# A tuned two-network transformer kernel whose instruction order is set with the timeline simulator's timing model

## The chip, the cores and the metric

The kernel runs on one core of one Trainium2 chip. The time is that of one execution on the device, in microseconds (us). A core has five engines that run side by side, each its own list of instructions in a fixed order: TensorE for matrix products (PE; its weight loads are PEld), VectorE (DVE), ScalarE (ACT), GpSimd (POOL) and SyncE (SP), which here issues nearly all transfers from the chip's memory (DMA). An engine that reaches an instruction whose input is not there yet stands still; it never takes a later one first. So the order in each list is a part of the program.

## The reference, cut to what matters

A sequence of 256 rows of 1024 numbers goes through two networks, one after the other, in fp32.

```python
def first_block(x, positions, ...):            # two layers
    for i in range(DEPTH):
        x = x + 0.5 * swiglu_ffn(x, ffn1_norm[i], ffn1_w_gate[i], ffn1_w_up[i], ffn1_w_down[i])
        h = rmsnorm(x, mix_norm[i])
        if i % 2 == 0:
            x = x + even_mixer(h, ...)         # chunked gMLP; attention over compressed,
        else:                                  # selected and windowed keys
            x = x + odd_mixer(h, ...)          # attention over indexed keys; attention over blocks
        x = x + 0.5 * swiglu_ffn(x, ffn2_norm[i], ...)
    return rmsnorm(x, final_norm)

def second_block(x, c, ...):
    mod = silu(c) @ w_ada + b_ada
    h = modulate(rmsnorm_2(x, g_mix), sh1, sc1)
    proj = h @ w_in
    y_a = rwkv7_time_mix(h, proj[..., :o1], ...)
    y_b = rglru_branch(proj[..., o1:o2], proj[..., o2:o3], ...)
    merged = sigmoid(proj[..., o3:o4]) * (y_a @ p_a) + sigmoid(proj[..., o4:]) * (y_b @ p_b)
    x = x + gt1 * (merged @ w_out)
    h2 = modulate(rmsnorm_2(x, g_ffn), sh2, sc2)
    x = x + gt2 * hier_moe(h2, ...)            # 32 experts, two for each row
    return modulate(rmsnorm_2(x, g_final), shf, scf)
```

In the RG-LRU branch the gates are `gate_r = sigmoid(...)` and `gate_i = sigmoid(...)`, and the input of the recurrence carries `sqrt(-expm1(2.0 * log_a))`: tanh, exp and sqrt alternate there.

## The kernel before, in words

Activations lie transposed in SBUF, 128 features by 256 tokens in a tile. A weight matrix comes in pieces of 128x1024 or 128x2048 fp32 numbers into a stage tile `s` by a DMA on SP (line 353); ACT rounds it to a high part `h` (helper `act`, line 258), DVE forms the low part `l = s - h` (helper `tt`, line 239), and a product is three matmuls, `xh*h`, `xl*h` and `xh*l`, where `xh` and `xl` are the two parts of the activations (`mm`, line 233; `tr`, line 236, is a transpose on PE). All helpers have one line each, so a row of the profile is told apart by its tiles: `ps` is a PSUM bank, `we` an expert's weights, `con` constants.

The stages, by the times of the trace: FFN 1 of layer 0 to about 207 us; the even mixer to 345; FFN 2 and FFN 1 of layer 1 to 757; the odd mixer to 881; FFN 2 to 1076; then the second network: the input projection with the RWKV part's preparation (`rwkv_in`, lines 1337 and on) to 1197, among it the RG-LRU gates (`rglru`, lines 1307 to 1335) at 1197 to 1218; the RWKV recurrence in blocks (`rwkv_out`) to 1317; merge and output projection to 1345; router and experts (`moe_round`, line 1898) to about 1585; the last norm to 1600. Weights of the modulation (`ada`, on DVE) are folded in beside the FFNs.

In the mixers and in the second network, code of two kinds is written as generators and interleaved: latency chains (attention units, RWKV units, where each step on PE waits for ACT, DVE or POOL) and plain products of weights ("fillers"), which give PE work meanwhile. In the even mixer the fillers are `blocks` B(0) and B(1) (`ps<-s,ev_blkk` and `ps<-s,ev_blkv`), features F(4) to F(6), and gMLP (line 851).

In `rwkv_in` each of the four units starts with a product of `tw` and `w2a` and, after a chain through ACT, POOL and DVE (a norm by `pow` on POOL, then `ex4` on DVE, line 455), has `ex4` broadcast by PE, `ps<-con,ex`.

In `rglru` every channel group c has two products into banks of one tag (p1), two Tanh that read them (`gr`, `gi`), an Exp and a Tanh, and then a Sqrt of `gr` (line 1328). Sqrt stands in another table of ACT than Tanh and Exp, and a switch is an instruction of ACT, ACT_TABLE_LOAD.

The experts: their 1 MB pieces `we` are loaded by SP in the order of use, into a ring of buffers; a load whose buffer is still read by PE waits on SP. For the experts that are ordered by their number of rows, the address comes from a table `moe_idx` in SBUF, read into registers of SP ahead of the load (line 1863, in `expert_load`):

```python
            if (p, kind) not in self.where:
                self.where[p, kind] = self.nc.sync.value_load(self.idx[0:1, p:p + 1], min_val=0, max_val=NEXP - 1)
            e = bass.ds(self.where[p, kind], 1)
            src = self.A["w2e"][e].squeeze(0) if kind else self.A["w13"][e, h].squeeze(0)
```

Each such read is a TENSOR_LOAD and two register instructions behind it. 48 of them are executed.

Nothing in the kernel writes the order of a list out by hand, but for a few `issue_after` hints (as that at the end of `rglru`, which keeps the Gelu behind the last Sqrt). The program is written down as one sequence of operations with their tiles, and the framework's scheduler (`tile.TileContext`) makes the list of every engine from it: it walks through the operations with a model of how long each takes, and puts next on an engine what is ready first by that model. By default it uses its own table of costs.

## Time and profile before

| | us |
|---|---|
| median of 2 runs | 1599.16 (1596.77 and 1601.55) |
| profiled execution | 1602.33 |
| its span from first to last instruction | 1600.6 |
| PE busy | 1533.1 |
| DVE / ACT / POOL busy | 1049.0 / 696.7 / 320.6 |

The prediction rests on views of the one profiled execution. The page gives the busy time of each engine, the span in 40 slices, and the chain of work that ended last, followed back from the end. A view by windows gives, for each stretch, the time each engine was busy, with the number of its instructions, the clock that TensorE was granted (1.00 is 2.4 GHz, 0.50 is 1.2 GHz), the mean busy share of the 16 DMA engines, and the bytes per second. The waits view sums what an engine stood waiting for. A timeline lists instructions one after another (neighbours of one kind in one row, with their count), and in brackets the idle time ahead of one and what ended it. The length shown for a matmul runs to its modelled end; matmuls overlap, so that the distance from start to start is what one costs.

### The profile page before, as it was taken

What the parts mean: (1) busy time and instruction counts of PE and PEld (TensorE: products, weight loads), DVE (VectorE), ACT (ScalarE), POOL (GpSimd) and SP (SyncE); (2) the same over time, 40 slices, a digit from 0 to 9 for tenths busy, and PEclk for the clock granted to TensorE, in tenths of its full rate; (3) what the DMA queues carried; (4) which work ended last, traced back from release to release, by engine and by line L of the source; (5) the groups of instructions that cost most, each with busy time, mean ns of one, the idle gap of its engine ahead of it and who ended that gap; (6) DMA issues with size and microseconds to landing.
All of it is one profiled execution on the core that took longest, in us unless ns stands there. A gap on an engine that the chain in (4) does not pass through costs nothing.

```text
span 1600.6 us, 29956 instructions
## 1 busy us (share of the span) xinstructions
PE 1533.1 (96%) x11925; PEld 1361.7 (85%) x11925; DVE 1049.0 (66%) x1938; ACT 696.7 (44%) x1241; POOL 320.6 (20%) x338
## 2 busy tenths in 40 slices
PE   8999998999999999999999999999899999999976
PEld 8999996789999999999878999998898889644433
DVE  6777876776875667766897678757786556532212
ACT  5544444554454444444545445534456433211102
POOL 4222222132220112201221222224313013000000
PEclk9999999999999999999999999999999999999997
DMA  8675555035774657745433576536440139899995
GB/s 305 241 281 199 197 196 193 27 120 204 270 253 162 211 184 263 262 166 185 145 110 132 205 269 243 189 119 227 133 148 27 54 141 378 323 388 420 420 421 193
DMA packets 62484, 344.35 MB, mean 215 GB/s; under 512 B 11137, under 2 KB 15361, under 8 KB 28545
## 3 DMA queue, kind: packets, MB, share of 16 engines
q1 hardware_dynamic: 59520, 340.65, 57.9%
q8 instruction: 96, 1.57, 0.4%
q0 software_dynamic: 640, 1.57, 0.4%
q10 hardware_dynamic: 2176, 0.13, 0.1%
q14 instruction: 52, 0.42, 0.1%
HBM read 339.05 MB, written 2.36 MB: 213 GB/s over the span
## 4 chain that ended last, share of the span: by engine, by line
PE 71%; issue 15%; DVE 8%; POOL 2%; ACT 2%; DMA 1%; ACTq 0%; SPq 0%; DVEq 0%; POOLq 0%
PE ps L233 70%; DVE l L239 2%; PE ps L236 1%; ACT h L258 1%; DVE xl L248 1%; POOL rte L239 1%; DVE t L239 1%; POOL t L239 0%; DVE xh L243 0%; DMA s<-in_ffn_gu 0%; DMA s<-in_ev_win 0%; DVE t L248 0%; POOL sq L239 0%; POOL kne L239 0%; DVE x L239 0%
## 5 line engine op out<-in xcount | busy, mean ns | idle before, releaser
L233 PE MATMUL ps<-xh,h 128*128 128x256 f32 x1992 | 570.1, 286 | 12.3 <-ACT h L258 7.6
L233 PE MATMUL ps<-xh,l 128*128 128x256 f32 x1992 | 570.4, 286 | 0.0
L233 PE MATMUL ps<-xl,h 128*128 128x256 f32 x1992 | 568.9, 286 | 0.3
L258 ACT ACTIVATE h<-s 128x1024 fp32r<-128x1024 f32 (+4 forms) x419 | 401.5, 960 | 366.9 <-PE ps L233 289.1
L239 DVE TENSOR_TENSOR l<-s,h 128x1024 fp32r<-128x1024 f32 (+4 forms) x416 | 464.9, 1125 | 139.5 <-ACT h L258 138.3
L233 PEld LDWEIGHTS ps<-xh,h 128*128 128x128 f32 x1992 | 380.8, 191 | 17.2 <-ACT h L258 7.0
L233 PEld LDWEIGHTS ps<-xh,l 128*128 128x128 f32 x1992 | 380.8, 191 | 6.1 <-DVE l L239 2.7
L233 PEld LDWEIGHTS ps<-xl,h 128*128 128x128 f32 x1992 | 381.1, 191 | 1.4 <-DVE xl L248 0.9
L233 PE MATMUL ps<-ah,h 128*128 128x256 f32 x704 | 201.4, 286 | 0.0
L239 POOL TENSOR_TENSOR t<-t,t 128x256 f32<-128x256 f32 x93 | 121.1, 1303 | 399.6 <-DVE t L239 338.8
L233 PE MATMUL ps<-ah,l 128*128 128x256 f32 x704 | 199.3, 283 | 0.1
L233 PE MATMUL ps<-al,h 128*128 128x256 f32 x704 | 199.1, 283 | 0.0
L233 PEld LDWEIGHTS ps<-ah,l 128*128 128x128 f32 x704 | 134.9, 192 | 0.4 <-DVE l L239 0.3
L233 PEld LDWEIGHTS ps<-al,h 128*128 128x128 f32 x704 | 135.0, 192 | 0.0
L233 PEld LDWEIGHTS ps<-ah,h 128*128 128x128 f32 x704 | 134.9, 192 | 0.0
L233 PE MATMUL ps<-we,gT 128*32 128x512 f32 (+1 forms) x512 | 100.1, 610 | 7.7 <-DMA we<-in_w 7.7
L239 DVE TENSOR_TENSOR t<-ps,rb 128x256 f32<-128x256 f32 x196 | 81.9, 421 | 33.1 <-PE ps L233 25.0
L258 ACT ACTIVATE ah<-t 128x256 fp32r<-128x256 f32 x88 | 36.7, 417 | 117.6 <-POOL t L239 117.6
L239 DVE TENSOR_TENSOR al<-t,ah 128x256 fp32r<-128x256 f32 x88 | 38.0, 432 | 63.9 <-ACT ah L258 63.9
L233 PEld LDWEIGHTS ps<-we,gT 128*32 128x32 f32 (+1 forms) x512 | 26.0, 121 | 59.9 <-issue 44.7
L239 POOL TENSOR_TENSOR sa<-sa,sq 128x256 f32<-128x256 f32 x34 | 41.9, 1232 | 149.7 <-ACT sq L258 149.4
L248 DVE SCALAR_TENSOR_TENSOR ada<-s,ca,ada 128x1024 f32<-128x1024 f32 x56 | 71.5, 1278 | 0.0
(487 smaller groups left out, 2091.1 us busy)
## 6 DMA issues: line engine op xcount, KB each, us to landing
s<-in_ffn_gu SPq DMA_DIRECT2D x87, 1024.0 KB
we<-in_w SPq DMA_DIRECT2D x64, 1024.0 KB
s<-in_ffn_dn SPq DMA_DIRECT2D x64, 704.0 KB
we<-in_w2e SPq DMA_DIRECT2D x28, 1024.0 KB
s<-in_w_ada SPq DMA_DIRECT2D x24, 1024.0 KB
s<-in_w_in SPq DMA_DIRECT2D x18, 1024.0 KB
s<-in_w_ada_f SPq DMA_DIRECT2D x8, 1024.0 KB
s<-in_ev_win SPq DMA_DIRECT2D x7, 1024.0 KB
```

The costliest lines, as they stand in the source:

```text
L233: return self.nc.tensor.matmul(out, lhsT, rhs, start=start, stop=stop, skip_group_check=True)
L236: self.nc.tensor.transpose(out, in_, ident)
L239: return (eng or self.nc.vector).tensor_tensor(out, a, b, op=op)
L248: self.nc.vector.scalar_tensor_tensor(out, a, s, b, op0=op0, op1=op1)
L258: self.nc.scalar.activation(out, a, f, **kw)
```

## The change

One argument is added: the scheduler takes the time of each operation from the framework's other timing model, that of the timeline simulator, instead of its own table. The operations stay the same; their order in the lists of all five engines is made anew.

```diff
-    with tile.TileContext(nc) as tc:
+    with tile.TileContext(nc, schedule_with_timeline_sim=True) as tc:
```

PE, DVE, POOL and SP execute the same instructions as before in another order; ACT has four more, all ACT_TABLE_LOAD. Three places show how.

On PE at the start of the second network's RWKV units (`rwkv_in`): `m_tw,m_w2a` are the first products of unit 0, `xh,h`, `xl,h` and `xh,l` are products of input features that need none of it. Rows with + are the order now, with - the order before.

```order
 L233 MATMUL ps_13606<-xl_13358,h_13598 128x256
 L233 MATMUL ps_13606<-xh_13394,l_13599 128x256
+L233 MATMUL ps_13744<-m_tw,m_w2a 128x256
+L233 MATMUL ps_13750<-m_tw,m_w2a 128x256
 L233 MATMUL ps_13638<-xh_13359,h_13602 128x256
 L233 MATMUL ps_13638<-xl_13358,h_13602 128x256
@@ -8122,6 +8123,4 @@
 L233 MATMUL ps_13712<-xl_13358,h_13676 128x256
 L233 MATMUL ps_13712<-xh_13394,l_13677 128x256
-L233 MATMUL ps_13744<-m_tw,m_w2a 128x256
-L233 MATMUL ps_13750<-m_tw,m_w2a 128x256
 L233 MATMUL ps_13833<-xh_13359,h_13825 128x256
```

The two products stand 72 feature matmuls earlier. The broadcast that ends this unit's chain, `ps_13765`, stood inside the feature `ps_13833`, 25 instructions behind the products; now it stands here, behind the next feature:

```order
 L233 MATMUL ps_13859<-xl_13358,h_13829 128x256
 L233 MATMUL ps_13859<-xh_13394,l_13830 128x256
+L233 MATMUL ps_13765<-con,ex_2534_13766 128x128 x2
+L233 MATMUL ps_13819<-t_2550_13817,con 128x256
 L233 MATMUL ps_13895<-xh_13359,h_13887 128x256
 L233 MATMUL ps_13895<-xl_13358,h_13887 128x256
```

Between the second product and the broadcast lie 122 instructions of PE instead of 24. In the other three units the distance grows from 35 to 68, from 81 to 116, and from 24 to 50.

On ACT in `rglru`: `gi` and `gr` are the gates, L1328 is the Sqrt.

```order
 L258 ACTIVATE xb_13582<-gr_13574,nsp_12282 128x256
-L258 ACTIVATE gi_13578<-ps_14932,hb_igate 128x256
 L258 ACTIVATE t_2767_14937<-gr_13574,sp_12281 128x256
 L1328 ACT_TABLE_LOAD
 L1328 ACTIVATE gr_13573<-gr_13573 128x256
+L258 ACT_TABLE_LOAD
+L258 ACTIVATE gi_13578<-ps_14932,hb_igate 128x256
+L1328 ACT_TABLE_LOAD
 L1328 ACTIVATE gr_13574<-gr_13574 128x256
 L258 ACT_TABLE_LOAD
 L258 ACTIVATE gr_13575<-ps_14947,hb_rgate 128x256
```

The second gate's Tanh has moved between the Sqrt of group 0 and that of group 1, so that the table is switched four times for the two Sqrt instead of twice; the same happens a little later between groups 2 and 3.

On SP in the queue of the experts' loads, before the change:

```order
L1873 DMA we_17410<-in_w 128x2048
L1873 ISA
L1873 DMA we_17412<-in_w 128x2048
L1873 ISA
L1873 DMA we_17414<-in_w 128x2048
L1873 DMA we_17467<-in_w2e 128x2048
L1873 DMA we_17469<-in_w2e 128x2048
L1863 TENSOR_LOAD moe_idx
L1863 ISA x2
L1873 ISA
L1873 DMA we_17486<-in_w 128x2048
```

and with it, from the end of the reads between `we_17412` and `we_17469`:

```order
L1863 TENSOR_LOAD moe_idx
L1863 ISA x2
L1873 DMA we_17469<-in_w2e 128x2048
L1863 TENSOR_LOAD moe_idx
L1863 ISA x2
```

The reads, which were spread over the whole queue, come in blocks: 15 between `we_17408` and `we_17410`, 11 between `we_17412` and `we_17469`, 5 between this and `we_17414` (then `we_17467` and `we_17486`), 12 between `we_17486` and `we_17497`, one more ahead of `we_17552`; the remaining four are the first of all, and stand as before.

## Rows read from the trace of the kernel before

**Rows 1.** The page: busy time of each engine, and the chain by engine.

```profile
PE 1533.1 (96%) x11925; PEld 1361.7 (85%) x11925; DVE 1049.0 (66%) x1938; ACT 696.7 (44%) x1241; POOL 320.6 (20%) x338
PE 71%; issue 15%; DVE 8%; POOL 2%; ACT 2%; DMA 1%; ACTq 0%; SPq 0%; DVEq 0%; POOLq 0%
```

**Rows 2.** Windows: start:end, length, each engine's busy time, clock, DMA share, GB/s.

```profile
100.00:200.00 100.00, 100.00 (x836) 99.73 (x834) 76.86 (x133) 45.28 (x69) 22.57 (x14) 1.00 0.62 216
245.00:337.00 92.00, 85.23 (x607) 64.64 (x606) 67.36 (x186) 46.85 (x147) 15.75 (x17) 0.98 0.27 97
778.00:890.00 112.00, 105.61 (x797) 91.10 (x798) 93.48 (x228) 60.01 (x139) 24.68 (x26) 0.98 0.35 123
1090.00:1197.00 107.00, 99.25 (x777) 93.99 (x777) 81.10 (x171) 47.40 (x83) 32.04 (x48) 0.97 0.49 165
1197.00:1218.00 21.00, 18.75 (x101) 14.43 (x99) 16.20 (x37) 18.70 (x37) 6.55 (x15) 0.84 0.09 15
1287.00:1317.00 30.00, 29.90 (x261) 26.16 (x261) 15.12 (x48) 11.26 (x26) 4.11 (x4) 1.00 0.39 139
1317.00:1345.00 28.00, 23.82 (x181) 23.19 (x181) 20.89 (x33) 11.52 (x18) 9.46 (x8) 0.94 0.93 360
1404.00:1527.00 123.00, 121.07 (x766) 58.06 (x762) 31.68 (x80) 18.75 (x35) 0.00 (x0) 1.00 1.01 420
1527.00:1575.00 48.00, 38.61 (x213) 14.80 (x217) 8.24 (x21) 4.25 (x8) 0.00 (x0) 0.96 1.02 414
```

**Rows 3.** Timelines of ACT, DVE and PE: one weight piece in an FFN.

```profile
28.96 1.06 ACT L258 ACTIVATE h<-s 128x1024 fp32r<-128x1024 f32 x1 [0.40 <-PE ps L233]
34.57 0.28 PE L233 MATMUL ps<-xh,h 128*128 128x256 f32 x1
34.69 0.28 PE L233 MATMUL ps<-xl,h 128*128 128x256 f32 x1
```

**Rows 4.** Timeline of PE, even mixer: two neighbours of a block B.

```profile
263.62 0.38 PE L233 MATMUL ps<-s,ev_blkk 128*64 128x256 f32 x1
263.84 0.38 PE L233 MATMUL ps<-s,ev_blkk 128*64 128x256 f32 x1
```

**Rows 5.** Waits of PE at 1090 to 1197: total, times, longest.

```profile
PE ps L233 <- DVE ex L455: 6.2, 4, 1.8
```

**Rows 6.** Timeline of PE there, unit 0, and a window behind such a wait.

```profile
1103.69 0.70 PE L233 MATMUL ps<-m_tw,m_w2a 64*128 64x256 f32 x4
1109.72 0.68 PE L233 MATMUL ps<-con,ex 128*128 128x128 f32 x4 [1.80 <-DVE ex L455]
1110.00:1114.00 4.00, 4.00 (x22) 3.82 (x20) 3.92 (x7) 1.33 (x2) 1.91 (x1) 0.58 0.00 0
```

**Rows 7.** Timeline of ACT, RG-LRU.

```profile
1201.89 0.59 ACT L258 ACTIVATE t<-gr,sp 128x256 f32<-128x256 f32 x1
1202.50 1.28 ACT L1328 ACT_TABLE_LOAD   x1
1203.79 0.72 ACT L1328 ACTIVATE gr<-gr 128x256 f32<-128x256 f32 x2
1204.53 1.28 ACT L258 ACT_TABLE_LOAD   x1
```

**Rows 8.** Timeline of SP: issues of experts' loads.

```profile
1402.16 1.48 SPq L1873 DMA_DIRECT2D we<-in_w  x3
1403.87 2.93 SPq L1873 DMA_DIRECT2D we<-in_w2e  x2
1407.64 0.35 SPq L1873 DMA_DIRECT2D we<-in_w  x1
```

**Rows 9.** The table's reads, by line: ns least/median/most; then a window.

```profile
L1863 SPq TENSOR_LOAD <-moe_idx x48: 262/270/457, 1382.7 to 1550.3; - x48
1403.00:1404.00 1.00, 1.00 (x6) 0.29 (x4) 0.68 (x1) 0.00 (x0) 0.00 (x0) 1.00 0.92 139
```

**Rows 10.** Waits of PE at 1527 to 1575.

```profile
PE ps L233 <- DMA we<-in_w: 7.7, 6, 1.4
```

## The prediction

> **What bounds the kernel now.** I read the page first. PE is busy for 1533.1 us of the span of 1600.6, and it holds 71% of the chain that ended last [rows 1]. So the kernel ends when PE has done its list, and a new order can gain only the 67 us in which PE stands idle, and what its clock loses beside them. Where these lie the windows tell [rows 2]. In an FFN stretch (100 to 200 us) PE is busy for 100.00 of 100 us: nothing to gain, something to lose. The idle time sits in the mixed stages: 92.00 - 85.23 = 6.8 us in the even mixer, 6.4 in the odd one, 7.8 in the RWKV preparation, 2.3 in the RG-LRU stretch (with a granted clock of 0.84), 0.1 in the RWKV recurrence, 4.2 at merge and output projection. From 1404 on something else bounds: the DMA engines are full (share 1.01 and 1.02, 420 and 414 GB/s), PE has worked off its backlog at 1527 and then waits for experts' weights, 7.7 us in six waits [rows 2, 10]. There every microsecond in which the DMA engines stand idle is added to the end.
>
> **The change part by part.** It removes and adds no work but four table loads, and moves much. I went through the new lists stage by stage and asked of each move what then ends last.
>
> *FFNs, two thirds of the span.* In every second half of a weight piece the first two matmuls that need the next `h` stand 22 instructions earlier. One matmul costs 34.69 - 34.57 = 0.12 us from start to start, so they come 2.6 us earlier. ACT has `h` ready at 28.96 + 1.06 = 30.02 and PE uses it at 34.57, 4.5 us later [rows 3]. The move costs nothing: 1.9 us of margin are left. If that cover were gone, each piece would cost up to 2.6 us, many times over; I take it as covered, since PE is busy without a gap there now, and count 0. At the start, sums and squares move earlier, in front of a wait for the first weights that stays: 0.
>
> *Even mixer.* B(0) and B(1) and the feature F(4) now stand ahead of the attention units that they filled. B is 32 pairs at 263.84 - 263.62 = 0.22 us, 7.0 us [rows 4]; F(4) is 48 matmuls at 0.12, 5.8 us. Bounds: all 6.8 us of idle time gained; or the whole 12.8 us of cover lost. DVE is busy for 67.36 of 92 us, so the units' softmax chains have room, and features F(5) and F(6) stay between them. I take +3, nearer to the middle (12.8 - 6.8) / 2 = +3 than to an end.
>
> *Odd mixer.* The same kind of move with fewer fillers; DVE is busy for 93.48 of 112 us, which leaves its chains less room. Bounds -2 (a third of 6.4) to +5 (one F(4)-sized block uncovered); I take +1.
>
> *RWKV preparation.* Here the new order is better. Four times PE stands before `ps<-con,ex` until DVE has made `ex`, 6.2 us in all [rows 5]. In unit 0 the chain runs from the product at 1103.69 to the broadcast at 1109.72, 6.0 us, with 24 instructions in between [rows 6]; now 122 are between, 14 us at 0.12. In the others the distance grows by 33, 35 and 26 instructions, 4.0, 4.2 and 3.1 us, more than the longest wait, 1.8. Behind the first wait PE runs at clock 0.58, between the two levels of 1.2 and 2.4 GHz, for 4 us [rows 6]; at full clock that work takes 2.3, so the wait costs up to 1.7 more. Bounds: 0 (another operand of the chain comes later, as DVE and POOL have new orders too) to -7.9. I take -6, since all four distances exceed the chain.
>
> *RG-LRU.* Four more ACT_TABLE_LOADs of 1.28 us lie on ACT, 5.1 us [rows 7]. ACT is busy for 18.70 of the 21 us [rows 2], the tightest place that it has, and PE needs it to free the banks of the gates before the next products. A part is hidden, for the features that PE can do meanwhile. Bounds +1 and +6 (5.1 and a Tanh that waits behind); I take +3.
> Each load in the trace begins 0.02 us after the ACTIVATE ahead of it ends (1201.89 + 0.59 = 2.48) and lets the next start 0.01 us after it [rows 7]: a switch costs 1.28 us. The Trainium skill, ScalarE: Activation LUTs, "What ACT_TABLE_LOAD costs", has the same 1283 ns but adds some 1380 ns of DRAIN for every switch to another set; by that the four would cost 10.6 us and the term would be about +8. The trace shows no such drain, so the sum goes by the row.
>
> *RWKV recurrence.* Products of the merge (two features of 24 matmuls, 5.8 us) that filled its second half now run earlier, and the chain stands bare from about 1287. PE has 0.1 us of idle time there [rows 2], so little can be won and up to 5.8 lost; DVE is half idle (15.12 of 30). I take +2.
>
> *Merge and output projection.* Loads change places among themselves; the DMA engines are at 0.93 there and carry the same bytes [rows 2]. 0, from -3 to +3.
>
> *Experts.* The reads of the table come in blocks. Issues without a read between them are (1.48 - 0.33) / 2 = 0.58 us apart, where 0.33 is an issue's own length (0.35 in the third row); from the second issue of the second row (1403.87 + 2.93 - 0.33 = 1406.47) to the next, with one read between, it is 1.17 [rows 8]. So a read costs 0.6 us of SP, of which the TENSOR_LOAD itself is 0.27 [rows 9]; its own two register instructions follow each, in both orders. `we_17410` was issued at 1402.16 and the DMA engines were busy for 0.92 of the microsecond from 1403, so data flow about 1 us after an issue [rows 8, 9]. A piece of 1024 KB (1.05 MB) at 420 GB/s takes 2.5 us. With the change: the 15 reads (9 us) lie in a wait for a buffer that SP has anyway, before 1402. `we_17410` and `we_17412` keep the engines busy from 1403.1 to 1408.1. Then come 11 reads, 6.6 us, so `we_17469` is issued at 1409.7 and flows from 1410.7: 2.6 us idle. It lasts to 1413.2; five reads on, `we_17414` is issued at 1413.1 and flows from 1414.1: 0.9 idle. Three pieces last to 1421.6; 12 reads on, `we_17497` is issued at 1421.9 and flows from 1422.9: 1.3 idle. After that SP is ahead again. 4.8 us in all, and since the engines are full from 1404 to 1575, the end moves by as much. Bounds: 0, if PE comes to the first buffers earlier or the reads overlap; 8, if a second block misses its cover too. I take 4.8.
> The Trainium skill, DMA: Bandwidth & Descriptors, "Latency and other measured facts", gives a floor of about 600 ns for a `tensor_load` and says that reads are unrolled by four to amortize it. The 0.6 us of the rows agree with the floor; by the second half of the sentence a block would be cheaper than its single reads (a quarter, 1.7 us for 11) and the idle time near 0. No row shows two reads back to back.
>
> Sum: 0 + 3 + 1 - 6 + 3 + 2 + 0 + 4.8 = +7.8 us, against the profiled execution's own 1602.33: 1610.1. That execution is 3.2 us above the median of the two runs shown, 1599.16; against the median the sum gives 1607.
>
> **The rivals.**
> *Little happens.* The moves are nearly all hidden: FFN 0, mixers 0, RWKV preparation -3, RG-LRU +1, DMA gaps +3: about 1600. For it speaks that PE has work queued in most stages, against it that the three costs have each a place that is tight now.
> *Not slower.* One mechanism, the blocks of reads: if reads that stand back to back overlap (a quarter of 0.6 us each), the stream has no gap and the term of 4.8 falls away; it decides where 11 reads take less than the 5.4 us between the issue of `we_17412` at 1402.7 and the end of its data at 1408.1, less 1 us for the start, so less than 0.4 us a read. With the full gain of 7.9 in the preparation instead of 6 the sum is then +1.1, and with the even mixer at 0 instead of +3, -1.9: 1597. That each read is followed by its own register instructions speaks against it.
> *Slower by far.* Front-loaded fillers: in the even mixer, the odd mixer and the recurrence the chains stand bare, 12.8 + 5 + 5.8 = 23.6 us, and after each wait the clock falls as it does at 1110 (1.7 us each, some five times more, 8 us). With RG-LRU +6 and the DMA gaps, and the preparation's gain of 6 kept, this is 23.6 + 8 + 6 + 4.8 - 6 = +36: 1636. It decides where a unit's step on ACT and DVE takes longer than what is left between two units on PE. For it speaks that these chains set the order now; against it that DVE and ACT are not full.
> *The table switch with a drain* is a part of this: +5.5 on the forecast, about 1613.
>
> **How the numbers follow.** Chances: the forecast with its own spread of 1600 to 1618, 0.50 (0.05 of it the drain); little happens 0.17; not slower, 1585 to 1599, 0.15; slower by far, 1618 to 1650, 0.18, of which 0.11 lie above 2%. A measurement of this kernel can tell about 2%, 32 us, from no change; so faster by more than 2% (below 1567) would take half of all idle time of PE, 0.02, from the third; slower 0.11; within 2% 0.87. I leave out the lowest part of the third case and the upper half of the fourth: 1590 to 1628.
>
> **What would show it.** Right: in the preparation the wait for `ex` on line 455 is gone (below 1 us); eight table loads of 1.28 us around 1200 instead of four; SP issues with gaps of over 6 us behind `we_17412`, and there a window with a DMA share under 0.6 after 1408; the FFN windows stay at 100.00 of 100; the idle time in the mixers 2 to 5 us larger. Wrong: idle time of PE within an FFN, which I count at 0 and which would come many times over; or attention waits that double.

## The result, and the profile after

| | before | after |
|---|---|---|
| median of the runs, us | 1599.16 | 1613.42 (1611.39 and 1615.45) |
| ratio to before | | 1.009 (95% interval 1.0069 to 1.0112) |
| profiled execution / its span, us | 1602.33 / 1600.6 | 1615.45 / 1613.6 |
| mean granted clock | 0.982 | 0.979 |

The kernel became 14 us slower; the forecast was 1607 in a range of 1590 to 1628. The sign is right and the size is near. The way there is not: the terms of the sum missed by up to 11 us each, in both directions.

The page of the changed kernel, busy time by engine and the chain by engine, to be held against [rows 1]:

```profile
PE 1539.4 (95%) x11925; PEld 1363.3 (84%) x11925; DVE 1074.8 (67%) x1938; ACT 700.8 (43%) x1245; POOL 313.8 (19%) x338
PE 70%; issue 16%; DVE 8%; ACT 3%; DMA 2%; POOL 0%; SPq 0%; ACTq 0%; DVEq 0%; POOLq 0%
```

POOL has left the chain (2% before), ACT and DMA have gained a point each. To find where the time went, I matched TensorE's matmuls in the two traces by the names of their tiles, and took the delay of after against before at places where the same matmuls lie ahead in both orders. The differences from place to place are what each stage won or lost:

| stage (time in the trace of before) | forecast | measured, us |
|---|---|---|
| start, to 37 | 0 | +2.9 |
| FFNs (37-193, 371-562, 577-743, 886-1064) | 0 | -5.1 |
| first products of three FFNs, with the norm's: 352-371, 562-577, 863-886 | not listed | -9.6 |
| even mixer, 244-337 | +3 | +1.4 |
| odd mixer, 783-863 | +1 | +2.1 |
| RWKV preparation, 1108-1164 | -6 | -11.2 |
| RG-LRU, 1164-1218 | +3 | +6.7 |
| RWKV recurrence, 1218-1315 | +2 | +12.7 |
| merge, output projection and router, 1315-1377 | 0 | +5.7 |
| experts, 1377-1585 | +4.8 | +8.3 |
| the rest | 0 | -0.1 |
| sum | +7.8 | +13.8 |

The sum ends at the experts' last product; the last norm gives 0.8 us back, so that the two spans differ by 13.0. The start and the even mixer vary between executions of one order, by about 3 us each, and RG-LRU with the recurrence by as much. With that margin, the order won 26 us in some places and lost 40 in others.

**What it won.** In the FFNs, a window of before (start:end, length, busy time of PE, PEld, DVE, ACT and POOL with their instructions, clock, DMA share, GB/s):

```profile
400.00:500.00 100.00, 100.00 (x832) 98.92 (x831) 76.03 (x101) 47.98 (x70) 22.60 (x16) 1.00 0.67 241
```

and of after:

```profile
400.00:500.00 100.00, 100.00 (x846) 100.00 (x844) 79.33 (x102) 48.21 (x70) 24.25 (x16) 1.00 0.69 241
```

PE is busy all the time in both, yet does 14 matmuls more in the second. The reason shows in the timelines of DVE, of the weight loads (PEld) and of PE of before:

```profile
422.09 0.43 DVE L239 TENSOR_TENSOR al<-t,ah 128x256 fp32r<-128x256 f32 x1 [1.08 <-ACT ah L258]
422.44 1.28 DVE L248 SCALAR_TENSOR_TENSOR ada<-s,ca,ada 128x1024 f32<-128x1024 f32 x1
423.63 0.42 DVE L239 TENSOR_TENSOR t<-ps,rb 128x256 f32<-128x256 f32 x1
423.96 2.35 DVE L239 TENSOR_TENSOR l<-s,h 128x1024 fp32r<-128x1024 f32 x2
425.23 0.19 PEld L233 LDWEIGHTS ps<-xh,l 128*128 128x128 f32 x1 [0.15 <-DVE l L239]
425.01 0.28 PE L233 MATMUL ps<-xl,h 128*128 128x256 f32 x1
425.23 0.39 PE L233 MATMUL ps<-xh,l 128*128 128x256 f32 x1
425.46 0.28 PE L233 MATMUL ps<-xh,h 128*128 128x256 f32 x1
```

and DVE's with the change:

```profile
419.16 2.96 DVE L248 SCALAR_TENSOR_TENSOR ada<-s,ca,ada 128x1024 f32<-128x1024 f32 x2
422.04 1.21 DVE L239 TENSOR_TENSOR l<-s,h 128x1024 fp32r<-128x1024 f32 x1
423.18 0.41 DVE L239 TENSOR_TENSOR al<-t,ah 128x256 fp32r<-128x256 f32 x1
```

Before, DVE stood 1.08 us for `ah` in front of `al` and came late to the next weights' low half `l`; PE's starts then came 0.22 apart instead of 0.12, twice. With the change `l` stands ahead of `al`. In the four FFN stretches there are 74 distances between 0.18 and 0.27 us in before and 36 in after; at 0.1 us each, that is some 4 of the 5.1. A matmul's shown length of 0.28 reaches over such a gap: the busy time can't show it.

Where an FFN begins, the norm's factor `rte`, a power on POOL, is spread over the columns by a product on PE. At the first of three such places before, timelines of PE, DVE and POOL, and then a window behind them:

```profile
365.93 0.71 PE L233 MATMUL ps<-con,rte 128*128 128x128 f32 x4 [1.56 <-POOL rte L239]
364.07 1.23 DVE L239 TENSOR_TENSOR l<-s,h 128x1024 fp32r<-128x1024 f32 x1
364.08 1.80 POOL L239 TENSOR_TENSOR rte<-rtt,mhalf 128x2 f32<-128x2 f32 x1 [3.54 <-DVE rtt L243]
```

the window:

```profile
366.00:371.00 5.00, 5.00 (x30) 5.00 (x31) 1.18 (x3) 2.08 (x3) 0.73 (x1) 0.66 0.12 48
```

and after, POOL and DVE, then the same window:

```profile
367.25 0.72 POOL L239 TENSOR_TENSOR rte<-rtt,mhalf 128x2 f32<-128x2 f32 x1 [2.88 <-DVE rtt L243]
367.47 2.36 DVE L239 TENSOR_TENSOR l<-s,h 128x1024 fp32r<-128x1024 f32 x2 [0.31 <-ACT h L258]
```

the window:

```profile
366.00:371.00 5.00, 5.00 (x44) 5.00 (x44) 2.59 (x4) 3.17 (x4) 0.72 (x1) 1.00 0.34 77
```

PE stood 1.56 us, and then ran at 0.66 of its clock: 30 matmuls in 5 us instead of 44. With the change the product stands 26 matmuls behind the sums instead of 4 (28 at the third place), and no wait for `rte` is left at the three places.

In RWKV's preparation the wait for `ex` [rows 5] is 1.0 us, once, and the clock holds through the first three of the four pairs. The row of the waits in after:

```profile
PE ps L233 <- DVE ex L455: 1.0, 1, 1.0
```

and the window:

```profile
1099.00:1144.00 45.00, 45.00 (x372) 43.56 (x371) 37.44 (x67) 21.87 (x40) 22.90 (x28) 1.00 0.48 164
```

**What it lost.** RG-LRU: the eight table loads came (1187.99 to 1204.94, 1.28 us each), and behind them `b_th`, for which PE stood. A window of after, then PE's timeline:

```profile
1144.00:1209.00 65.00, 53.94 (x370) 47.83 (x369) 47.79 (x112) 39.40 (x67) 11.16 (x21) 0.89 0.28 91
```

the timeline:

```profile
1208.47 0.39 PE L233 MATMUL ps<-xh,h 128*128 128x256 f32 x1 [3.40 <-ACT b_th L258]
```

Recurrence: 12.7 us. Of them, 3.4 are that wait for `b_th`, and 3.0 are lost in the 13 us behind it, while the clock is reduced (0.83 from 1208 to 1218). The rest, some 6 to 7 us, lies between there and the end of the stage. At the end of the stage, the window of before:

```profile
1305.00:1317.00 12.00, 11.93 (x87) 10.95 (x86) 8.60 (x29) 5.00 (x9) 4.11 (x4) 1.00 0.58 225
```

and of after:

```profile
1305.00:1317.00 12.00, 10.69 (x50) 8.16 (x50) 7.46 (x25) 2.52 (x5) 4.14 (x4) 0.72 0.31 96
```

Router: SP now has six more loads of experts' weights ahead of the eight reloads of `x`, 12 instead of 6. After, timelines of SP, DVE and PE, then a window:

```profile
1315.96 3.22 SPq L1873 DMA_DIRECT2D we<-in_w  x6
1329.12 12.73 SPq L1152 DMA_DIRECT2D xr<-xd  x6
1346.95 0.88 DVE L248 SCALAR_TENSOR_TENSOR xr<-ps,mod,xr 128x256 f32<-128x256 f32 x2 [7.86 <-DMA xr<-xd]
1348.14 1.07 PE L233 MATMUL ps<-pre_wr,b_u 128*128 128x36 f32 x4 [4.91 <-DVE b_u L243]
```

the window:

```profile
1343.00:1367.00 24.00, 19.09 (x134) 18.87 (x134) 10.51 (x18) 6.71 (x11) 4.50 (x5) 0.79 0.76 288
```

Before, the eight reloads were issued from 1321.92 to 1328.55; here the last two follow at 1346.54.

Experts: the DMA engines, full from 1404 on before [rows 2], go short twice. Windows over the same two stretches of work, of before:

```profile
1404.00:1420.00 16.00, 16.00 (x82) 6.57 (x78) 3.32 (x8) 1.76 (x3) 0.00 (x0) 1.00 1.01 422
1420.00:1440.00 20.00, 20.00 (x156) 11.83 (x156) 7.88 (x22) 4.05 (x8) 0.00 (x0) 1.00 1.01 421
```

and of after:

```profile
1411.00:1427.00 16.00, 16.00 (x84) 7.21 (x81) 4.59 (x11) 3.52 (x6) 0.00 (x0) 1.00 0.81 296
1427.00:1447.00 20.00, 20.00 (x144) 8.99 (x146) 6.60 (x17) 3.66 (x7) 0.00 (x0) 1.00 0.92 365
```

At 421 GB/s the missing bytes are 16 x (1 - 296/421) = 4.8 and 20 x (1 - 365/421) = 2.7 us, 7.4 together; the end moves by 8.3.

The blocks of reads are there as forecast, and at their forecast price. SP and its reads behind `we_17412`, issued at 1408.80, in after, and the DMA engines behind them:

```profile
L1863 SPq TENSOR_LOAD <-moe_idx x11: 263/263/274, 1409.2 to 1414.8; - x11
1415.45 0.34 SPq L1873 DMA_DIRECT2D we<-in_w2e  x1
1414.00:1418.00 4.00, 4.00 (x20) 1.29 (x18) 1.17 (x2) 1.64 (x3) 0.00 (x0) 1.00 0.58 174
```

Reads that stand back to back start 0.56 us apart and do not overlap, no load is issued for 6.3 us, and the share falls to 0.58. Whether this is what the end loses, only a run can tell.

### The profile page after: what moved, and what is told of

The parts are those of the page before. It is cut to its first block, busy times and chain, and to the rows that moved or that the text cites. A ratio compares the mean times of both kernels' runs of the same rounds, so it can differ in the third digit from the quotient of the medians.

```text
span 1613.6 us, 29989 instructions
## 1 busy us (share of the span) xinstructions
PE 1539.4 (95%) x11925; PEld 1363.3 (84%) x11925; DVE 1074.8 (67%) x1938; ACT 700.8 (43%) x1245; POOL 313.8 (19%) x338
## 4 chain that ended last, share of the span: by engine, by line
PE 70%; issue 16%; DVE 8%; ACT 3%; DMA 2%; POOL 0%; SPq 0%; ACTq 0%; DVEq 0%; POOLq 0%
PE ps L233 69%; DVE l L239 2%; PE ps L236 1%; DMA xr<-xd 1%; ACT h L258 1%; DVE t L239 1%; DMA s<-in_ev_win 0%; ACT L1328 0%; ACT L258 0%; DVE t L248 0%; DMA s<-in_pab 0%; DMA s<-in_w_in 0%; DVE xl L1089 0%; DMA x<-in_xT 0%; DVE xl L248 0%
## 5 line engine op out<-in xcount | busy, mean ns | idle before, releaser
L239 DVE TENSOR_TENSOR l<-s,h 128x1024 fp32r<-128x1024 f32 (+4 forms) x416 | 473.3, 1140 | 158.8 <-ACT h L258 157.6
L233 PE MATMUL ps<-xh,l 128*128 128x256 f32 x1992 | 561.4, 285 | 0.5 <-DVE l L239 0.5
L233 PEld LDWEIGHTS ps<-xh,l 128*128 128x128 f32 x1992 | 377.0, 190 | 1.9 <-DVE l L239 1.3
L233 PE MATMUL ps<-we,gT 128*32 128x512 f32 (+1 forms) x512 | 104.5, 611 | 8.0 <-DMA we<-in_w 7.6
L248 DVE SCALAR_TENSOR_TENSOR ada<-s,ca,ada 128x1024 f32<-128x1024 f32 x56 | 82.7, 1519 | 0.0
L239 POOL TENSOR_TENSOR sa<-sa,sq 128x256 f32<-128x256 f32 x34 | 37.5, 1103 | 153.7 <-ACT sq L258 153.2
L239 POOL TENSOR_TENSOR rte<-rtt,mhalf 128x2 f32<-128x2 f32 x10 | 8.1, 809 | 284.0 <-DVE rtt L243 283.9
```

What stands on the lines that cost most here:

```text
L233: return self.nc.tensor.matmul(out, lhsT, rhs, start=start, stop=stop, skip_group_check=True)
L239: return (eng or self.nc.vector).tensor_tensor(out, a, b, op=op)
L248: self.nc.vector.scalar_tensor_tensor(out, a, s, b, op0=op0, op1=op1)
```

## The experiments

Each kernel was timed against the kernel before on the same chip, in three rounds. In us, a ratio of 0.001 is 1.6; the change alone is 1.009. A difference between two rows carries both intervals, some 4 to 6 us either way.

| kernel | median, us | ratio, 95% interval |
|---|---|---|
| after_reads | 1615.41 | 1.0085 (1.0063 to 1.0106) |
| after_sqrt | 1608.14 | 1.0057 (1.0036 to 1.0077) |
| after_xr | 1607.13 | 1.0042 (1.0028 to 1.0056) |
| after_out | 1612.96 | 1.0082 (1.0065 to 1.0099) |
| after_loads | 1614.69 | 1.0100 (1.0065 to 1.0136) |
| after_w2a | 1616.38 | 1.0102 (1.0064 to 1.0140) |
| after_tail | 1613.88 | 1.0085 (1.0058 to 1.0112) |
| before_norm | 1590.32 | 0.9947 (0.9929 to 0.9965) |
| after_pieces | 1608.17 | 1.0047 (1.0033 to 1.0062) |
| before_rw | 1598.66 | 0.9995 (0.9981 to 1.0009) |
| after_sum | 1597.77 | 0.9985 (0.9973 to 0.9997) |
| before_three | 1585.22 | 0.9901 (0.9881 to 0.9921) |

**The experts: reads, loads, pieces.** First the theory of the prediction.

```diff
-                self.where[p, kind] = self.nc.sync.value_load(...)
+                with ExitStack() as es:
+                    if self.lastwe is not None:
+                        es.enter_context(self.tc.issue_after(self.lastwe.ins))
+                    self.where[p, kind] = self.nc.sync.value_load(...)
```

> The changed kernel, with each read of the experts' table queued behind the load ahead of it, so that SP's list is as before the change in the experts' part; all other lists stay as in the changed kernel. If the blocks of reads starve the DMA engines, as the sum had it and as the trace after shows from 1404 on (the delay against before grows from +5.4 to +13.7 us there), about 8 us come back: 1605. If the delay comes from PE's later arrival at the buffers, 1613 stays.

1.0085: nothing came back. The gap behind the block did go; the window of after_reads over the same time:

```profile
1414.00:1418.00 4.00, 4.00 (x22) 1.31 (x20) 1.03 (x2) 1.07 (x2) 0.00 (x0) 1.00 0.95 360
```

But SP now stands before the loads instead: between 1376 and 1450 it waits 37.3 us for PE's reads of the loaded pieces, 22.1 in after. The DMA engines go short a little later (share 0.83 from 1428 to 1448; 0.92 in after from 1427 to 1447). The blocks of reads lay in waits that were there anyway, so they are not what the end loses. The next suspect was the order of the loads on SP.

```diff
+    def behind(self):
+        return self.tc.issue_after(self.lastwe.ins) if self.lastwe is not None else ExitStack()
...
-            self.nc.sync.dma_start(t, src)
+            with self.behind():
+                self.lastwe = self.nc.sync.dma_start(t, src)
...
-            n_more = nc.values_load(nxi[0:1, 0:1], min_val=0, max_val=3)
+            with self.behind():
+                n_more = nc.values_load(nxi[0:1, 0:1], min_val=0, max_val=3)
```

> The changed kernel with SyncE's list put back in the experts' part: each expert load and each table read is queued behind the load that is written ahead of it, and the read of the number of further passes (nxi) behind the last load. In the changed kernel nxi stood ahead of the load we_17228 and held SyncE for 9.9 us, and a load of a w2 half stood ahead of loads whose buffers were free; the experts' part lost 8 us between 1493 and 1524 although queueing the reads alone gave nothing. If the order of the loads is the cause: 1613.4 - 8 = about 1605.5, and the DMA engines idle again about 8 us of 1376 to 1560 instead of 18. If the loss lies in the order of TensorE's or VectorE's work in the experts: 1613 again, and the delay still grows by 8 us between 1493 and 1524.

1.0100: this falls too; the delay still grows by 7.3 us from 1493 to 1524, and the DMA engines go short in the same place. Loads in order do not help if the rooms come free out of order. In the traces, PE has read the 9th and 10th piece by 1401.5 before, when the 11th to 14th are not yet done; in after_loads it has read them by 1409.6, when the 11th to 14th, the 17th and the 18th are done (the last of them at 1406.2). Rooms are handed out in load order, so the load that waits for the 9th room holds SP and all loads behind it. The third run adds to after_loads an order for PE:

```diff
+        def piece(*a):
+            with self.tc.issue_after(prev[-1].ins) if prev else ExitStack():
+                prev.append(self.mm(*a))
+            return prev[-1]
...
-                    self.mm(ph[i * cap:(i + 1) * cap, :], gT[4 * h + k][:, c:c + cap], ...)
+                    piece(ph[i * cap:(i + 1) * cap, :], gT[4 * h + k][:, c:c + cap], ...)
```

> The changed kernel with SyncE's list as in after_loads and, besides, each product that reads an expert's weights queued behind the product that is written ahead of it, so that TensorE uses the loaded pieces in the order in which they were loaded, as the kernel before nearly does (the changed kernel uses the 17th to 20th piece ahead of the 9th, 10th, 15th and 16th, and two pieces of the next round before two older ones; a piece's room is given to a load in load order). SyncE alone gave nothing. If rooms that come free out of order are what the experts lose: the 7 to 8 us between 1493 and 1524 go, 1605 to 1607, and in after_loads' rows the three longest waits of SyncE for TensorE shrink (15.2 us the longest; 10.7 before). If the loss has another cause in the experts: 1613 again.

1.0047: 8.5 us less than after_loads. In the experts the delay grows by 1.8 us instead of 8.8. Windows of after_loads:

```profile
1404.00:1420.00 16.00, 16.00 (x85) 7.34 (x82) 4.72 (x11) 3.52 (x6) 0.00 (x0) 1.00 0.76 287
1420.00:1440.00 20.00, 20.00 (x147) 8.88 (x149) 6.58 (x17) 3.66 (x7) 0.00 (x0) 1.00 0.90 359
```

and of after_pieces, which reaches the same work some 4 us later:

```profile
1408.00:1424.00 16.00, 16.00 (x85) 6.54 (x81) 3.33 (x8) 1.76 (x3) 0.00 (x0) 1.00 1.01 419
1424.00:1444.00 20.00, 18.79 (x148) 11.01 (x147) 7.31 (x21) 4.04 (x8) 0.00 (x0) 1.00 1.01 415
```

So the order in which PE uses the pieces, with the loads in order, is what the experts lost. Whether PE's order alone would do, with SP's list as the change made it, wasn't tried.

**RG-LRU's table loads.**

```diff
-            self.act(th, gr[c], AF.Tanh, ...)
+            tanh = self.act(th, gr[c], AF.Tanh, ...)
...
-            last = nc.scalar.activation(gr[c], gr[c], AF.Sqrt)
+            with self.tc.issue_after(tanh.ins):
+                last = nc.scalar.activation(gr[c], gr[c], AF.Sqrt)
```

> The changed kernel, with the Sqrt of the RG-LRU part queued behind the last Tanh of its gates: four table loads there, in two pairs, instead of eight. If the loads on ACT are what holds PE there (PE waits 4.4 us for a gate's input at 1193 and 3.4 us for ACT at 1208 in the trace after), 5 to 8 us come back: 1605 to 1608. If the units of the recurrence that were moved into this stretch are the cause, less than 2: 1612.

1.0057, 5.3 us less than the change. Four loads of 1.28 us, 5.1 us, are gone, and PE's wait for `b_th` shrinks from 3.4 to 2.5 us. From 1164 to 1315 the delay grows by 14.2 us; in after and four other runs that leave this stretch as it is, by 16.6 to 20.1.

**The reloads of x.**

```diff
-                            nc.sync.dma_start(self.x[k], self.xd[:, k])
+                            self.xr = nc.sync.dma_start(self.x[k], self.xd[:, k])
...
-        self.expert_ahead()
+        with self.tc.issue_after(self.xr.ins):
+            self.expert_ahead()
```

> The changed kernel, with the six loads of experts' weights that it had put ahead of the eight loads of the residual (xr) queued behind them again. The trace after has DVE wait 7.9 us for xr and PE 4.9 us behind it at 1348, with the clock lowered for some us after. If the order on SP is the cause, 5 to 7 us come back: 1606 to 1608. If the DMA engines are full there in any order and the router is late anyway, 1613 stays.

1.0042, 7.7 us less. About 4 of them lie in the router's stage, where the delay grows by 1.5 us instead of 5.3; the rest is within the spread of stages that the edit doesn't touch. DVE no longer waits for `xr<-xd`, and the router runs at full clock. Its window in after_xr:

```profile
1336.00:1360.00 24.00, 22.77 (x192) 21.90 (x191) 11.79 (x25) 6.98 (x13) 4.36 (x6) 1.00 0.94 375
```

**The recurrence, twice.** First the fillers kept as written, then only the last 24 of them moved back.

```diff
-        self.mm(out, wh, xh, first, False)
+        m = self.mm(out, wh, xh, first, False)
+        if first and self.pin:
+            self.tc.keep_in_program_order(m)
```

> The changed kernel, with every filler feature in the RWKV recurrence pinned behind what is written ahead of it, so that the fillers are spread again. Between 1218 and 1315 of before the same 847 matmuls take 97.2 us, in the changed kernel 106.3 us with the last 10 us at a clock of 0.66. If the front-loaded fillers are the cause, 5 to 9 us come back: 1604 to 1608. If the waits come from elsewhere, pinned fillers only add waits: 1613 or more.

1.0082: nothing in the time. But the loss has moved. Pinned, 216 of the 240 fillers are spread over the recurrence, and there the delay doesn't grow: -12.3 us at 1233 and at 1305 of before, where after loses 7.1 from 1233 to the end of the stage. The last 24 stand behind the norms, which run bare from 1286.7 to 1307, and from 1305 to 1317 of before the delay grows by 7.4. The window of after_out:

```profile
1292.00:1307.00 15.00, 13.70 (x72) 10.98 (x68) 8.72 (x28) 3.80 (x7) 4.08 (x4) 0.71 0.40 146
```

```diff
-                    for k in range(4):
-                        self.mm3(p[:, :S], *w((d % 4 * 4 + k) * P), *yl[k], k == 0, k == 3)
+                    with self.tc.issue_after(self.tail.ins) if d > 5 else ExitStack():
+                        for k in range(4):
+                            self.mm3(p[:, :S], *w((d % 4 * 4 + k) * P), *yl[k], k == 0, k == 3)
```

> The changed kernel with the last 24 filler matmuls of RWKV's recurrence (the products ps_3048 and ps_3049, second projection, column blocks 6 and 7) queued behind the first product of the norms at the end, where the kernel before has them (1305 to 1313), instead of at 1285 to 1289. The norms' tail ran bare in the changed kernel: 1301.9 to 1317.8 without a filler, at clock 0.66, where the kernel before took 12.4 us with the 24 fillers inside. If the bare tail is what the recurrence loses: 3 us of fillers move into waits and the clock stays up, so 3 to 6 us less, 1607.5 to 1610.5, with the clock at 0.9 or more between 1305 and 1315. If the loss lies earlier (the products at 1217 to 1290 being spread thinner): 1613, and the delay grows as much by 1318.

1.0085: nothing either. The scheduler put the 24 as two blocks right behind the first norm's product, and the last norms still ran bare. The end of the stage in after_tail:

```profile
1300.00:1313.00 13.00, 12.40 (x66) 10.44 (x65) 9.14 (x27) 2.52 (x5) 4.10 (x4) 0.67 0.28 92
```

The kernel before has them in seven portions of 1 to 9 between the norms' steps, and keeps clock 1.00. That spreading is what counts is argued from these windows and from after_out's first part; no run had all fillers spread, the norms' 24 among them.

**The norm's product**, undone on the side of the kernel before:

```diff
                 elif f == 0:
-                    rb, _ = self.rstd()
+                    e, rbs = self.rstd_tok(), []
+                    up(1, lambda end: rbs.append(self.rstd(e, end)[0]))
+                    rb, = rbs
...
-        pb = self.bcast(e)
+        with self.tc.issue_after(end.ins) if end else ExitStack():
+            pb = self.bcast(e)
```

> The kernel before, with one edit: in an FFN that no staged weights lead into, the product that spreads the norm's rte over the columns is queued behind the first half of the second piece, 24 matmuls later, as the changed kernel has it (it stood 4 matmuls behind the sums). Three places: 365.9, 564.5 and 881.8. If the wait for GpSimd's power (1.5 us each) and the half clock behind it are what the changed kernel won at these boundaries (4.3, 3.5 and 1.9 us there): 1599.2 - 9.7 = 1589.5, with 1.00 of the clock right behind each place. If only the wait itself goes: 1599.2 - 4.6 = 1594.6. If the gain there had another cause: 1599.

0.9947, 8.5 us less than before (5.6 to 11.4): the wait and the half clock behind it, as expected; in the traces 3.3, 3.5 and 3.6 us at the three places.

**RWKV's preparation: what has to be far from what.**

```diff
-        self.mm(p[:, :S], w2a[0:64, cc], tw[0:64])
+        self.tc.keep_in_program_order(self.mm(p[:, :S], w2a[0:64, cc], tw[0:64]))
```

> The changed kernel with the two w2a products of each head pair kept where they are written, so that they stand 28, 15, 40 and 21 rows ahead of the sums of squares instead of 82, 32, 80 and 26 (before: 8, 25, 73, 26). From the sums to the product with ex there are 65, 44, 58 and 13 rows (changed kernel 38, 36, 34, 26; before 15, 9, 7, 22). By the reason in my prediction (the distance from w2a hides the chain) the waits for ex come back, 4 to 6 us of them, and with the half clock behind them RWKV's preparation loses 6 to 10 us: 1619 to 1623. By the rival reason (the distance from the sums to ex) only the last pair waits, some 1.5 us: 1613 to 1615, with TensorE at the full clock through 1099 to 1144.

1.0102, 2 us over the change and within its spread. Through the first two pairs PE is busy for 30.00 of the 30 us from 1100 to 1130, at clock 1.00, though w2a stands late, and there is no wait for `ex`; the last pair has one, of 0.8 us. (From 1092 to 1148 of before this run gains 8.0 us, the changed order 8.3; by 1232 it is 1.3 us behind that order, 0.9 of which it was at 1092.) So the distance from w2a is not what counts. The other side of it:

```diff
         en = self.rsqrt_tok(pss[:, 0:4], 1e-12, 4, "kn")
-        pk = self.bank("p3")
-        self.bcast_heads(pk, en)
+        with fill():
+            pk = self.bank("p3")
+            self.bcast_heads(pk, en)
```

> The kernel before, with one edit in RWKV's preparation: of the 48 gate products that are written behind each head pair, the first 24 now come between the sums of squares and the product with ex, which is queued behind them: 42, 35, 42 and 35 rows lie between the sums and ex instead of 15, 9, 7 and 22, while the w2a products stay 8, 15, 8 and 15 rows ahead of the sums. By the distance from the sums, three of the four waits for ex (6.2 us in all) and the half clock behind them go: 6 to 11.5 us less, 1588 to 1593. By the distance from w2a, on which my prediction built: about 1599, since w2a stands no earlier.

0.9995: neither theory. The wait for `ex` is gone, and one of nearly its size in all stands one link further down the chain. Waits of PE in the preparation of before_rw, the largest two:

```profile
PE ps L233 <- DVE rw_bk L239: 5.2, 4, 2.3
PE ps L233 <- DVE t L248: 2.2, 3, 1.1
```

`ex` leads over DVE (`kkh`, `bk`) to the next product, A0. The first pair's sums, `ex` and A0 start at 1105.43, 1109.72 and 1114.82 before, at 1104.53, 1109.99 and 1115.72 in before_rw, at 1097.59, 1102.55 and 1108.74 after. Each half of the chain takes 4.3 to 6.2 us, some 35 to 50 matmuls at 0.12. In PE's list 15 and 18 rows lie in the two halves before, 41 and 25 in before_rw, 38 and 46 after: only the new order covers both. Before, the second half had no wait to show: its 18 rows, at the reduced clock behind the first wait, lasted the whole 5.1 us.

The time as a whole hides two parts. Through the first three pairs, to 1165 of before, before_rw gains 4.5 us; the fourth pair waits 2.3 us for `rw_bk`, its clock falls, and by 1218 all is lost again. Windows of before and of before_rw:

```profile
1170.00:1180.00 10.00, 10.00 (x86) 9.55 (x85) 8.41 (x19) 4.00 (x6) 1.19 (x2) 1.00 0.39 125
1170.00:1180.00 10.00, 7.72 (x46) 7.50 (x47) 5.54 (x13) 1.33 (x2) 1.19 (x2) 0.66 0.35 110
```

**The sums.**

```diff
+ the edits of after_sqrt, after_xr, after_loads and after_pieces together
```

> The changed kernel with its named losses undone together: Sqrt behind the last Tanh (5.3 us back alone), six expert loads behind the reloads of x (6.3 back alone), SyncE's list of the experts and the pieces in load order (7 to 8 expected together). If they are separate: 1613.4 - 19 = 1594, under the kernel before, with the stretches up to 1164 as in the changed kernel. If one gain eats the other (an earlier router only waits longer for the loads): 1600 to 1602.

0.9985, 16.8 us less than the change, of 5.3 + 7.7 + 6.9 = 19.9 singly: nearly separate. The rest is given back in the experts, where the delay now grows by 4.3 us instead of 1.8.

```diff
+ the edits of before_norm and before_rw, and in the FFNs:
+                for n in (f + 1, f + 2):
+                    if f and n < NFF and n not in ps:
+                        up(n)
-                m.append(self.split_a(mm, mp, f"m{f}"))
+                with self.tc.issue_after(self.lo[0].ins):
+                    m.append(self.split_a(mm, mp, f"m{f}"))
```

> The kernel before with the three things that the changed order gained, written out by hand: the norm's product 24 matmuls later (9.4 us alone), ex behind the first half of the gate products (6 to 11.5), and in the FFNs the low half l of the next piece but one queued ahead of al on VectorE, so that TensorE does not wait for it (27 pairs of gaps, 5 us). If all three are what the trace of the changed kernel shows: 1599.7 - 9.4 - 9 - 5 = about 1576 (1572 to 1582). If the late l hides nothing or the new order of VectorE brings a wait of its own: 1579 to 1585.

0.9901, 15.8 us less than before: the fastest of all, with 30 late distances in the FFNs instead of 74; its four FFN stretches take 684.7 us instead of 691.1. It was expected at 1576; the 9 us of before_rw are missing, as that run shows by itself. Its two other parts give 1599.7 - 9.4 - 5 = 1585.3.

## Why the prediction was right, and where it was not

*Bound.* PE's list sets the end, and the experts are bound by the DMA engines: this held. The step "a new order can gain only the 67 us in which PE stands idle" had a hole: busy time runs to a matmul's modelled end, so "100.00 of 100 us" does not mean that nothing is to be gained. The FFNs won 5.1 us there, by 0.1 us at a time. The margin of `h`, 1.9 us, on which I counted 0, held; what I didn't look at was `l`.

*FFN starts.* I took the stages' boundaries for part of the FFNs and gave them no term. POOL's 2% of the chain [rows 1], gone after, were the sign. With the clock behind them they cost 9.6 us, more than any gain I listed.

*Preparation.* The place and the sign were right, the reason was not: I measured the distance from w2a, and in after_w2a that distance didn't matter. What the rows bear out is a chain that starts at the sums, passes `ex` and goes on to A0. As to size, I allowed 1.7 us for the clock behind a wait, once; it was -11.2, beyond my bound of -7.9.

*RG-LRU.* The four loads came, with 1.28 us each, and taking them away gave back 5.3. The estimate of +3 assumed that half is hidden; the stage lost 6.7, since the products behind it wait as well. The Trainium skill, ScalarE: Activation LUTs, "What ACT_TABLE_LOAD costs", would have made it 10.6 with a drain for each switch: neither the rows of after nor the run bear that out.

*Recurrence.* The mechanism was named (fillers run early, the chain stands bare), and sized at +2 with a bound of 5.8. It was +12.7: the wait for `b_th` with the clock behind it, 6.4 us, fell into it, and the norms ran bare at clock 0.72. That the bare chain is the rest is likely after after_out, but no run got it back.

*Router.* "Loads change places among themselves; 0" was wrong. I compared bytes, and not which of them a consumer waits for first: the reloads of `x`, issued 7 to 19 us later.

*Experts.* +4.8 against +8.3, for the wrong reason. The price of a read was right (0.56 us against 0.6, and no overlap, so the rival *not slower* fell), and the signs that I named came: over 6 us between issues, and a share of 0.58. Yet after_reads took the blocks away and nothing changed, nor with the loads in order: the step that failed is "the end moves by as much". The loads waited for rooms behind the reads, and it was PE's own order, which I had not followed to the rooms that it frees.

*Mixers.* +3 and +1 forecast, +1.4 and +2.1 measured: right within what one execution tells. No run took their moves apart.

That the sum came near is luck: three gains that I missed or undersized (5.1 + 9.6 + 5.2 = 19.9 us) met losses that I missed or undersized (10.7 + 5.7 + 3.7 + 3.5 = 23.6). Of the rivals, *slower by far* named bare chains that lose clock; the traces show that in the recurrence alone.

## What to carry to other kernels

Where an order is made anew, follow every buffer that is handed out in a ring: the order in which the consumer frees the rooms bounds the loads as much as the order in which they are issued. A latency chain needs cover in each of its links, so count the rows between every two of them; with the cover moved to the first link, the wait moved to the second. And where a scheduler's new order wins in some stages and loses in others, take the winning moves over by hand: the kernel before with three such moves, one of which brought nothing, ran at 0.990, while the new order with its losses undone ran at 0.9985.

## What the runs showed of the hardware

The waits of about 1.5 us for POOL cost 3.3 to 3.6 us each (before_norm): behind the first PE ran at 0.66 of its clock for the 5 us from 366 to 371. In the recurrence's end no gap of PE reaches 1 us, and the clock was 0.72 all the same.

The same power on POOL took 1.80 us where it began together with DVE's `l` (364.08 and 364.07), and 0.72 where it began 0.22 us ahead of it. At the places 364.08, 562.70 and 880.00 it is 1.80, 1.79 and 1.78, each next to an `l` of 1.23 us. The Trainium skill, SBUF — State Buffer, "SBUF: two separate sides", says that GpSimd and a VectorE instruction with two inputs from SBUF share a pair of ports that whoever starts first holds for its whole instruction. The trace agrees as to POOL: 0.72 and most of the 1.23 make the 1.80, and an `l` that begins later leaves POOL its 0.72. It doesn't show the other side: the `l` that began during POOL's 0.72 took 1.23 as well.
